# Splits, weight loads and zeros moved to other queues and places at four stage borders of a two-layer encoder kernel

## The chip, the cores and the metric

The kernel runs on one core of one Trainium2 chip. The metric is the device time of one execution in microseconds (us), taken as the median of several runs. A core has TensorE (PE, matmuls; PEld in the profile is its loading of the stationary operand), VectorE (DVE), ScalarE (ACT), GpSimd (POOL), and SyncE (SP), which only issues transfers (DMAs). Each engine works through its own queue of instructions in order and waits on semaphores for the others. Transfers issued by SP go to the queue that the profile calls q1, transfers issued by POOL to q0.

## The reference, cut to what matters

Two layers on x of 1024 tokens by 1024 channels, all in float32:

```
layer 0: h = LN(alpha*x + MLA(x));      h = LN(alpha*h + SwiGLU(h))
layer 1: h = LN(alpha*h + Diff(h));     h = LN(alpha*h + SwiGLU(h))

MLA:   c = x @ w_in; two RMS norms; q, k, v from the latents, a shared rotary key
       o = softmax(mask(q k^T * scale)) v, 8 heads;   o @ w_o
Diff:  q, k, v = h @ w_in; per head two softmax maps of 64 channels each
       a = softmax_0 - lam * softmax_1;  o = RMSnorm(a v) * g_sub * (1 - lambda_init);  o @ w_o
SwiGLU: (silu(gate) * up) @ w_down, 2816 hidden channels
```

The mask is causal by chunks of 64 tokens, and the differential attention has a penalty by distance.

## The kernel before, in words

**Products.** Every float32 operand of a matmul is split in two parts: hi is the value rounded to the matmul's format, lo is the rest. A product is three matmuls, hi·hi, hi·lo and lo·hi (`mm3`, L140). The hi part is a cast on ACT, the lo part a subtraction on DVE, or on POOL for weights. So whatever enters a product passes ACT first and then DVE or POOL. `load_w` (L128) does it for a weight: a transfer by SP into a raw tile, the cast at L136, the subtraction at L137 (POOL, if nothing else is asked for).

**Order.** The program is written as a list of Python calls, and a framework's scheduler, which has a time model of its own, sets the final order of each engine's queue. Two things hold it: a priority for some calls, and `behind(i, j)`, which forces instruction i to stand after j on the same engine, without a semaphore.

**Stages**, in order of time in the profile:

- *Start* (L927 to L1028). x comes transposed, in quarters for the first two blocks of 128 tokens (`load_x`); the eight row blocks of w_in come one after the other (`load_w_in`, the first in two pieces). `project` multiplies them as they come: hq (384 columns, L979) and hk (320 columns, L980). `ones`, a 128x128 constant that norms use later, is written by DVE at L1033.
- *Attention A* (L1051 to L1178). 8 heads by 8 blocks of 128 query rows; the last head takes its blocks in another order (6, 7, 4, 5, 2, 3, 0, 1, `LAST_ORDER`). For each block: scores on PE (s_a), row bounds on DVE (mx_a, L219), the exponential on ACT (L222), scaling by the row sum on POOL (l_a, L1137), transposes on PE (pt_a), their split (pth_a on ACT, L243, ptl_a on DVE, L244), and the product with the values (o_a, L255). The result goes to DRAM (o_dr).
- *out_proj 0* (L278). Eight weights wo0_0 to wo0_7 by `load_w`, and for each of eight token blocks: `of` from DRAM (eight heads by 128 columns), its split oh and ol (L302 on ACT, L303 on DVE), 48 matmuls (zp_a), residual and layer norm. Most weights are loaded during the attention; wo0_6 and wo0_7 come last.
- *FFN 0* (L486 on), whose end has a layer norm per token block: rs_f on POOL (L180), y_f on DVE (L176, L183), and transposes xTp_f on PE for layer 1.
- *Attention B* (L1203 to L1383), which starts in the shadow of FFN 0's end. Its two softmax maps lie on the two halves of the partitions, and the query tiles (bq, ql) must be zero where the other map's half is. Six quarter tiles of 64x512 that are never written otherwise (of bq1, ql0 and ql1) are zeroed once, by POOL, which subtracts the bias tile bb from itself (L1219). Each block of scores is two maps; l_b is scaled on POOL (L1281) and combined on DVE (L1282).
- *Output projection 1* (class `OutProj`, L325), interleaved with the last head of attention B. Its weights were split earlier and lie in DRAM (w_dr, in the profile wo_dr). `begin_out` (L1369) makes the object two blocks ahead of the last head: it loads `of` of the first block (6), then issues on POOL six loads of 1 MB (wo1_0 to wo1_5) and four of 512 KB (heads 6 and 7, into buffers shared with other weights). `of` (L349) loads six heads of a token block (384 KB in pieces of 512 bytes) and splits them: ACT at L377, DVE at L378; then it loads the residual z. A list (L1375) says in which block of attention B each piece is called: `early` products of the first block in slots 2 to 4, `of` of the second block (7) in slot 4, its `early` products in slots 6 and 7.
- *FFN 1* and the end.

Of the kernel before, what the change touches and what calls it, by code (L numbers as in the profile page):

```python
# [9 lines left out]
F32 = mybir.dt.float32  # L10
F32R = mybir.dt.float32r
# [31 lines left out]
def trunk(  # L43
# [57 lines left out]

    mhalf = cst[:, 0:2]
# [4 lines left out]
    def f32(t):  # L107
        return t.bitcast(F32)
# [15 lines left out]

    def small(name, n=1):
        return sp.tile([P, 2], F32, tag="small", name=name, bufs=22)[:, :n]

    def load_w(src, cols, name, hi=None, lo=None, eng=None, raw=None):  # L128
# [7 lines left out]
        A.copy(hi[:, :cols], raw[:, :cols])  # L136
        (eng or G).tensor_tensor(lo[:, :cols], raw[:, :cols], f32(hi[:, :cols]), ALU.subtract)  # L137
        return hi, lo
# [67 lines left out]
    def softmax_block(lp, q_pass, s_bias, i, scale, name):  # L206
        n = (i + 1) * P
        nb = 1 if n <= 512 else 2
        w = n // nb
        l = lp.tile([P, 1024], F32, tag="l", name=f"l_{name}")  # L210
        mx = BIGF
        for b in range(nb):
            s = ps_s(f"s_{name}_{b}")
            ks = slice(b * w, (b + 1) * w)
            for j, (lh, rh) in enumerate(q_pass):
                T.matmul(s[:, :w], lh, rh[:, ks], start=(j == 0), stop=(j == len(q_pass) - 1))
            bv = s_bias[:, 896 - P * i + b * w:896 - P * i + (b + 1) * w]
            m = small(f"mx_{name}_{b}")
            V.tensor_tensor_reduce(l[:, ks], s[:, :w], bv, -scale, mx, ALU.add, ALU.min, m)  # L219
            mx = m  # L220
        sm = small(f"sm_{name}")
        A.activation(l[:, :n], l[:, :n], AF.Exp, bias=mx, scale=-1.0, accum_out=sm)  # L222
        r = small(f"r_{name}")
        V.reciprocal(r, sm)  # L224
        return l, r

    def transpose_block(ptp, pts, l, i, name):
        qc = (i % 2) * P
        for jq in range(i // 4 + 1):
# [5 lines left out]
            for jp in range(2 * jq, 2 * jq + (nj + 1) // 2):  # L235
# [7 lines left out]
                A.copy(hv, src)  # L243
                V.tensor_tensor(lv, src, f32(hv), ALU.subtract)  # L244
# [33 lines left out]
    def out_proj(side, w_o, o_dram, x_src, x_dst, lng, lnb, xo):  # L278


        with tc.tile_pool(name="op0", bufs=2, side=side, reuse_waits="tile") as pool:
# [3 lines left out]
            for h in range(H):  # L285
# [7 lines left out]
                wo.append(load_w(w_o[h], 1024, f"wo0_{h}", *dst))  # L293
            prev = None
            for tb in LAST_ORDER:
# [6 lines left out]
                A.copy(oh, of)  # L302
                V.tensor_tensor(ol, of, f32(oh), ALU.subtract)  # L303
# [21 lines left out]
    class OutProj:  # L325
# [5 lines left out]
        def __init__(self, side, w_dr, o_dram, o_here, x_src, x_dst, scale):  # L331
# [4 lines left out]
            self.of(LAST_ORDER[0])  # L336
            self.wo = []
            for h in range(H):
                if h < self.HEADS:
                    t = self.pool.tile([P, 2, D], F32R, tag=f"wo{h}", name=f"wo1_{h}", bufs=1)  # L340
                    nc.gpsimd.dma_start(t, w_dr[h])
# [566 lines left out]

    o_dr = [[dr.tile([H, P, 256], F32, name=f"o_dr{l}_{g}") for g in range(4)] for l in range(2)]
    wo_dr = [dr.tile([P, 2, D], F32, name=f"wo_dr{h}") for h in range(H)]  # L910
# [122 lines left out]
    V.memset(ones, 1.0 / P)  # L1033
# [17 lines left out]
    with ast as st:  # L1051
# [76 lines left out]
        def score_a(h, i):  # L1128
# [8 lines left out]
            G.tensor_scalar(l[:, :n], l[:, :n], r, 1.0, ALU.mult, ALU.mult)  # L1137
# [39 lines left out]
        at(12, make_late)  # L1177
        attention(score_a, turn_a, mix_a, fill, 2, (0, 0))  # L1178
# [24 lines left out]
    with ExitStack() as st:  # L1203
# [11 lines left out]
        for ql in q_lo:  # L1215
            for mp in range(2):
                b = slice(64 - mp * 64, 128 - mp * 64)
                z = bb[b, :512]
                G.tensor_tensor(ql[b, mp * 512:mp * 512 + 512], z, z, ALU.subtract)  # L1219
# [258 lines left out]
```

## Time and profile before

| what | value |
|---|---|
| median of 3 runs | 2318.11 us (2317.43 to 2320.41) |
| the profiled execution, all of it | 2317.24 us |
| its span, first to last instruction | 2315.5 us |
| PE busy | 2253.4 us, 97% of the span |
| DVE, ACT, POOL busy | 67%, 44%, 39% |
| DMA queue of SP (q1) | 268.46 MB |
| DMA queue of POOL (q0) | 17.83 MB |

A row of a timeline gives the start and the length in us, engine and line, the operation, what it writes <- what it reads (buffer numbers left out: `wo` for wo1_3, and `s_b` for s_b7_7_0_0), the shape, how many such rows follow each other, and in brackets the idle time ahead of it and what ended it. "PE s_b <- DVE mx_b" reads: PE waited, ahead of a matmul into s_b, for DVE's mx_b. What ended a wait is inferred; where the named engine itself had been waiting for something, the cause lies one step further back.

### The profile page before, as it was taken

What the parts mean: (1) busy time and instruction counts of PE and PEld (TensorE: products, weight loads), DVE (VectorE), ACT (ScalarE), POOL (GpSimd) and SP (SyncE); (2) the same over time, 40 slices, a digit from 0 to 9 for tenths busy, and PEclk for the clock granted to TensorE, in tenths of its full rate; (3) what the DMA queues carried; (4) which work ended last, traced back from release to release, by engine and by line L of the source; (5) the groups of instructions that cost most, each with busy time, mean ns of one, the idle gap of its engine ahead of it and who ended that gap; (6) DMA issues with size and microseconds to landing.
All of it is one profiled execution on the core that took longest, in us unless ns stands there. A gap on an engine that the chain in (4) does not pass through costs nothing. (4 is left out here: it accounts for less than half of the span.)

```text
span 2315.5 us, 31126 instructions
## 1 busy us (share of the span) xinstructions
PE 2253.4 (97%) x11410; PEld 1918.7 (83%) x11410; DVE 1560.1 (67%) x2879; ACT 1018.5 (44%) x2092; POOL 891.9 (39%) x698
## 2 busy tenths in 40 slices
PE   9999999999999999999999999979999999999997
PEld 9898897888888887888888898967778888887886
DVE  5666664596666658677476766666596656658777
ACT  4466673352332324345465656545442333324343
POOL 2233351014444445465332423222014444436564
PEclk9999999999999999999999999989999999999999
DMA  5121335334323238454310202153344222337453
GB/s 202 41 91 69 106 101 178 125 142 145 125 76 129 86 119 322 182 183 140 101 46 31 71 25 69 37 191 111 126 144 149 99 103 102 113 129 303 146 203 121
DMA packets 103658, 288.29 MB, mean 125 GB/s; under 512 B 8528, under 2 KB 31696, under 8 KB 93008
## 3 DMA queue, kind: packets, MB, share of 16 engines
q1 hardware_dynamic: 98064, 268.46, 33.0%
q0 software_dynamic: 5440, 17.83, 2.3%
q8 instruction: 90, 1.47, 0.3%
q14 instruction: 64, 0.52, 0.1%
HBM read 205.00 MB, written 77.07 MB: 122 GB/s over the span
## 5 line engine op out<-in xcount | busy, mean ns | idle before, releaser
L469 ACT CAST op_g<-gr 128x512 fp32r<-128x512 f32 x240 | 147.5, 622 | 411.0 <-PE gb L514 228.3
L470 POOL TENSOR_TENSOR op_g<-gr,op_g 128x512 fp32r<-128x512 f32 x104 | 145.8, 1407 | 303.6 <-DVE tmp L605 153.6
L470 DVE TENSOR_TENSOR op_h<-rh,op_h 128x512 fp32r<-128x512 f32 x154 | 162.8, 1088 | 67.6 <-ACT op_h L469 67.6
L514 PE MATMUL ga<-xh_m,op_g 128*128 128x512 f32 x512 | 168.0, 389 | 0.0
L469 ACT CAST op_h<-rh 128x512 fp32r<-128x512 f32 x154 | 93.0, 619 | 145.0 <-PE dx L782 37.5
L782 PE MATMUL dw<-op_w_t,op_h 128*128 128x512 f32 x660 | 151.4, 390 | 0.0
L782 PEld LDWEIGHTS dw<-op_w_t,op_h 128*128 128x128 f32 x660 | 123.6, 188 | 25.9 <-DVE op_h L470 0.4
L222 ACT ACTIVATE l_b<-l_b,mx_b 128x256 f32<-128x256 f32 (+7 forms) x128 | 99.6, 778 | 76.2 <-DVE mx_b L219 74.2
L1281 POOL TENSOR_SCALAR l_b<-l_b,r_b,cst 128x128 f32<-128x128 f32 (+3 forms) x64 | 52.8, 825 | 205.1 <-DVE r_b L224 196.1
L470 POOL TENSOR_TENSOR op_w_t<-tt,op_w_t 128x512 fp32r<-128x512 f32 x66 | 98.8, 1501 | 77.1 <-ACT op_w_t L469 77.1
L782 PE MATMUL dx<-op_w_b,op_h 128*128 128x512 f32 x528 | 122.7, 392 | 5.9 <-ACT op_w_b L469 3.9
L782 PEld LDWEIGHTS dx<-op_w_b,op_h 128*128 128x128 f32 x528 | 98.3, 188 | 29.9 <-ACT op_w_b L469 4.7
L514 PE MATMUL gb<-t4h_f,op_g 128*128 128x512 f32 x352 | 115.8, 390 | 3.0 <-DVE tmp L597 3.0
L514 PE MATMUL gc<-b22h_f,op_g 128*128 128x512 f32 x352 | 115.6, 389 | 1.6 <-ACT op_g L469 1.6
L470 DVE TENSOR_TENSOR op_g<-gr,op_g 128x512 fp32r<-128x512 f32 x136 | 109.5, 807 | 9.0 <-ACT op_g L469 8.8
L514 PE MATMUL gc<-t1h_f,op_g 128*128 128x512 f32 x352 | 115.5, 389 | 0.0
L514 PE MATMUL gb<-t3h_f,op_g 128*128 128x512 f32 x352 | 115.2, 389 | 0.0
L514 PE MATMUL gb<-t2h_f,op_g 128*128 128x512 f32 x352 | 114.8, 389 | 0.0
L514 PEld LDWEIGHTS ga<-xh_m,op_g 128*128 128x128 f32 x512 | 96.1, 188 | 19.9
L470 POOL TENSOR_TENSOR op_g<-s,op_g 128x512 fp32r<-128x512 f32 x40 | 55.3, 1382 | 143.6 <-ACT op_g L469 143.6
L143 PE MATMUL bp<-xT_f,h_wb 128*128 128x512 f32 x256 | 103.4, 404 | 0.0
L145 PE MATMUL bp<-xT_f,l_wb 128*128 128x512 f32 x256 | 101.8, 398 | 0.0
(375 smaller groups left out, 6788.4 us busy)
## 6 DMA issues: line engine op xcount, KB each, us to landing
gr<-in_w_gu SPq DMA_DIRECT2D x44, 1024.0 KB, 6.7
rh<-h_dr SPq DMA_DIRECT2D x28, 1024.0 KB, 5.3
h_dr<-sh SPq DMA_DIRECT2D x22, 1024.0 KB, 4.9
h_dr<-hp SPq DMA_DIRECT2D x22, 768.0 KB, 4.1
tt<-in_w_dn SPq DMA_DIRECT2D x22, 512.0 KB, 7.5
rh<-h_dr SPq DMA_DIRECT2D x14, 768.0 KB, 4.3
z<-xs_dr SPq DMA_DIRECT2D x16, 512.0 KB, 10.0
rw_b<-in_w_dn SPq DMA_DIRECT2D x8, 1024.0 KB, 8.7
```

The lines of the kernel that those rows point to most:

```text
L143: T.matmul(ps_out, lh, rh, start=(i == 0), stop=False)
L145: T.matmul(ps_out, ll, rh, start=False, stop=(i == n - 1))
L222: A.activation(l[:, :n], l[:, :n], AF.Exp, bias=mx, scale=-1.0, accum_out=sm)
L469: A.copy(hi, src)
L470: eng.tensor_tensor(lo, src, f32(hi), ALU.subtract)
L514: T.matmul(o, w[:, a, kc], x[b][:, k, :], start=(first and k == 0 and (a, b) == (0, 0)), stop=(k == 3 and a == 1), skip_group_check=True,)
L782: T.matmul(o, h[:, a, c], w[:, b_], start=(first and (a, b_) == (0, 0)), stop=(last and a == 1), skip_group_check=True,)
L1281: G.tensor_scalar(l1[:, :n], l1[:, :n], r1, nlam, ALU.mult, ALU.mult)
```

## The change

1. *Start.* `ones` is written first thing on DVE. Eight matmuls of ones by ones into a score bank that nobody reads (`spin`) stand ahead of PE's first real matmul.
2. *End of attention A.* `load_w` can now hold the two halves of a split behind noted instructions: the splits of wo0_6 and wo0_7 stand behind the last exponential on ACT and the last scaling on POOL that were noted when the call was made. In out_proj 0 the split of each `of` is done in two halves of four heads, and those of the first block stand behind the last pth on ACT and the last ptl on DVE.
3. *Output projection 1.* `OutProj` loads `of` of both first blocks (6 and 7) before anything else, and all ten weight loads are issued by SP instead of POOL. The call of `of` for block 7 in slot 4 goes.
4. *Zeros.* In attention A (slot 14) ACT casts half a row of the zero part of ba into a tile, and SP stores it in DRAM (`zero_dr`). The six quarter tiles are filled by SP's transfers from there.

```diff
+    V.memset(ones, 1.0 / P)
...
+    def spin(n, name):
+        t = ps_s(name)
+        for i in range(n):
+            T.matmul(t[:, :P], ones, ones, start=True, stop=True)
...
+    newest = {}
+    def load_w(src, cols, name, hi=None, lo=None, eng=None, raw=None, after=()):
...
+        i = A.copy(hi[:, :cols], raw[:, :cols])
+        j = (eng or G).tensor_tensor(lo[:, :cols], raw[:, :cols], f32(hi[:, :cols]), ALU.subtract)
+        for k, key in zip((i, j), after):
+            behind(k.ins, newest[key])
...
-                wo.append(load_w(w_o[h], 1024, f"wo0_{h}", *dst))
+                wo.append(load_w(w_o[h], 1024, f"wo0_{h}", *dst, after=("exp", "scale") if h > 5 else ()))
...
-                A.copy(oh, of)
-                V.tensor_tensor(ol, of, f32(oh), ALU.subtract)
+                for hs in (slice(0, 4), slice(4, 8)):
+                    i = A.copy(oh[:, hs], of[:, hs])
+                    j = V.tensor_tensor(ol[:, hs], of[:, hs], f32(oh[:, hs]), ALU.subtract)
+                    if prev is None:
+                        behind(i.ins, newest["hi"])
+                        behind(j.ins, newest["lo"])
...
-            self.of(LAST_ORDER[0])
+            for tb in LAST_ORDER[:2]:
+                self.of(tb)
...
-                    nc.gpsimd.dma_start(t, w_dr[h])
+                    nc.sync.dma_start(f32(t), w_dr[h])
...
-                        nc.gpsimd.dma_start(t[p], w_dr[h][:, p])
+                        nc.sync.dma_start(f32(t[p]), w_dr[h][:, p])
...
+    spin(8, "spin0")
...
+        def store_zeros():
+            t = wp.tile([P, 1024], F32R, tag="wl", name="zeros")
+            A.copy(t[:, :512], ba[:, :512])
+            nc.sync.dma_start(zero_dr, f32(t[:, :512]))
+        at(14, store_zeros)
...
-                z = bb[b, :512]
-                G.tensor_tensor(ql[b, mp * 512:mp * 512 + 512], z, z, ALU.subtract)
+                nc.sync.dma_start(f32(ql[b, mp * 512:mp * 512 + 512]), zero_dr[b])
...
-            (4, "of", (second,)), (6, "early", (second, (0, 1, 2))), (7, "early", (second, (3, 4, 5))),
+            (6, "early", (second, (0, 1, 2))), (7, "early", (second, (3, 4, 5))),
```

`newest` notes the last instruction of a kind: "exp" at the exponential of `softmax_block`, "hi" and "lo" at the split in `transpose_block`, "scale" at POOL's scaling in attention A.

What this does to the queues, at three places. On SP where output projection 1 begins; before (of_a1_6 is the `of` of block 6; the weights stand on POOL):

```order
L1321 DMA o_dr1_3_88<-bo_10162 128x256
L354 DMA of_a1_6_15086<-o_dr1_3_88 128x6x128
L354 DMA of_a1_7_15420<-o_dr1_3_88 128x6x128
L354 DMA of_a1_4_15742<-o_dr1_2_87 128x6x128
L354 DMA of_a1_5_15833<-o_dr1_2_87 128x6x128
L372 DMA zy_a1_4_15747<-xs_dr1_98 128x1024
```

and after:

```order
L1346 DMA o_dr1_3_98<-bo_10191 128x256
L371 DMA of_a1_6_15115<-o_dr1_3_98 128x6x128
L371 DMA of_a1_7_15124<-o_dr1_3_98 128x6x128
L358 DMA wo1_0_15132<-wo_dr0_100 128x2048
L358 DMA wo1_1_15134<-wo_dr1_101 128x2048
L358 DMA wo1_2_15136<-wo_dr2_102 128x2048
L358 DMA wo1_3_15138<-wo_dr3_103 128x2048
L358 DMA wo1_4_15140<-wo_dr4_104 128x2048
L358 DMA wo1_5_15142<-wo_dr5_105 128x2048
L363 DMA who1_6_15144<-wo_dr6_106 128x1024
L363 DMA who1_7_15148<-wo_dr7_107 128x1024
L363 DMA wlo1_6_15145<-wo_dr6_106 128x1024
```

The ten weight loads have moved from POOL's queue into SP's, behind the second `of` and ahead of those of blocks 4 and 5.

On ACT at the end of attention A (pth_a7 are the last head's transposed weights, oh_a0_6 the first block's split of out_proj 0); before:

```order
L222 ACTIVATE l_a7_1_4545,sm_a7_1_4554<-l_a7_1_4545,mx_a7_1_0_4552 128x256
L136 CAST wo0_6_4670<-r_wo0_6_4671 128x1024
L243 CAST pth_a7_2_1_4541<-pt_a7_2_0_4533 128x128
L302 CAST oh_a0_6_4682<-of_a0_6_4680 128x1024
L243 CAST pth_a7_2_0_4537<-pt_a7_3_0_4559 128x2x128
L1147 COPY ob7_2_4516<-o_a7_2_4497 128x256
L243 CAST pth_a7_0_0_4586<-pt_a7_0_0_4584 128x128
L243 CAST pth_a7_0_0_4586<-pt_a7_1_0_4590 128x2x128
L243 CAST pth_a7_2_1_4541<-pt_a7_3_0_4559 128x2x128
L302 CAST oh_a0_7_4755<-of_a0_7_4753 128x1024
```

and after:

```order
L234 ACTIVATE l_a7_1_4558,sm_a7_1_4567<-l_a7_1_4558,mx_a7_1_0_4565 128x256
L146 CAST wo0_6_4683<-r_wo0_6_4684 128x1024
L146 CAST wo0_7_4688<-r_wo0_7_4689 128x1024
L255 CAST pth_a7_2_1_4554<-pt_a7_2_0_4546 128x128
L255 CAST pth_a7_2_0_4550<-pt_a7_3_0_4572 128x2x128
L1166 COPY ob7_2_4529<-o_a7_2_4510 128x256
L255 CAST pth_a7_0_0_4599<-pt_a7_0_0_4597 128x128
L255 CAST pth_a7_2_1_4554<-pt_a7_3_0_4572 128x2x128
L255 CAST pth_a7_0_0_4599<-pt_a7_1_0_4603 128x2x128
L315 CAST oh_a0_6_4695<-of_a0_6_4693 128x512 x2
L1166 COPY ob7_1_4594<-o_a7_1_4581 128x256
```

The first block's oh cast, now in two halves, has moved behind the last pth, and the cast of wo0_7 behind that of wo0_6. DVE's ol and ptl have moved alike, and on POOL both wo0 subtractions now stand behind the last l_a.

On POOL at the end of FFN 0; before:

```order
L137 TENSOR_TENSOR l_wb0_0_10304<-r_wb0_0_10301,h_wb0_0_10303 128x1024
L180 TENSOR_TENSOR rs_f0_0_10099<-ve_f0_0_10097,cst_63 128x1
L1219 TENSOR_TENSOR bq1_10159<-bb_10156 64x512 x2
L1219 TENSOR_TENSOR ql0_10163<-bb_10156 64x512 x2
L1219 TENSOR_TENSOR ql1_10164<-bb_10156 64x512 x2
L180 TENSOR_TENSOR rs_f0_1_10112<-ve_f0_1_10110,cst_63 128x1
```

and after:

```order
L147 TENSOR_TENSOR l_wb0_0_10333<-r_wb0_0_10330,h_wb0_0_10332 128x1024
L192 TENSOR_TENSOR rs_f0_0_10128<-ve_f0_0_10126,cst_63 128x1
L192 TENSOR_TENSOR rs_f0_1_10141<-ve_f0_1_10139,cst_63 128x1
L192 TENSOR_TENSOR rs_f0_2_10154<-ve_f0_2_10152,cst_63 128x1
L192 TENSOR_TENSOR rs_f0_3_10167<-ve_f0_3_10165,cst_63 128x1
```

The six zeros are gone from between the first and the second rs_f; SP's queue has six transfers in their place, two ahead of the load of bb and four behind it.

More of the change, by code (lines that the diff above doesn't have):

```diff
@@ L221, in softmax_block @@
         sm = small(f"sm_{name}")
-        A.activation(l[:, :n], l[:, :n], AF.Exp, bias=mx, scale=-1.0, accum_out=sm)
+        newest["exp"] = A.activation(l[:, :n], l[:, :n], AF.Exp, bias=mx, scale=-1.0, accum_out=sm).ins
         r = small(f"r_{name}")
@@ L242, in transpose_block @@
                 hv, lv = (t[:, :n, qc:qc + P] for t in pts[jp])
-                A.copy(hv, src)
-                V.tensor_tensor(lv, src, f32(hv), ALU.subtract)
+                newest["hi"] = A.copy(hv, src).ins
+                newest["lo"] = V.tensor_tensor(lv, src, f32(hv), ALU.subtract).ins
     def pv_group(pts, g, v_of, name):
@@ L907, in ffn @@
         return new, rest, normed
+    spin(8, "spin0")
     o_dr = [[dr.tile([H, P, 256], F32, name=f"o_dr{l}_{g}") for g in range(4)] for l in range(2)]
+    zero_dr = dr.tile([P, 512], F32, name="zero_dr")
     wo_dr = [dr.tile([P, 2, D], F32, name=f"wo_dr{h}") for h in range(H)]
@@ L1032, in trunk @@
     nlam = cst[:, 24:25]
-    V.memset(ones, 1.0 / P)
     lv = [late[:, 64 * i:64 * i + 64] for i in range(4)]
@@ L1136, in score_a @@
             n = (i + 1) * P
-            G.tensor_scalar(l[:, :n], l[:, :n], r, 1.0, ALU.mult, ALU.mult)
+            newest["scale"] = G.tensor_scalar(l[:, :n], l[:, :n], r, 1.0, ALU.mult, ALU.mult).ins
             lt[h, i] = l
```

3 lines of the change are left out of this document (removed).

## The prediction

> **What bounds the kernel now.** I read the page first, then the list of waits of TensorE, then the timeline of each engine around the longest waits, then the transfers there. The page's first part:
>
> ```profile
> PE 2253.4 (97%) x11410; PEld 1918.7 (83%) x11410; DVE 1560.1 (67%) x2879; ACT 1018.5 (44%) x2092; POOL 891.9 (39%) x698
> ```
>
> TensorE (PE) is busy 2253.4 of the span's 2315.5 us, so all its waiting is 62 us, and a change that leaves its matmuls alone can win only from that, or from time in which its clock is low. The waits, longest sums first (us in total, times, longest):
>
> ```profile
> PE s_b L216 <- DVE mx_b L219: 14.3, 1, 14.3
> PE hq L979 <- ACT wih L950: 4.3, 1, 4.3
> ...
> PE xTp_f L148 <- DVE y_f L183: 3.8, 2, 2.1
> ```
>
> These lie at places that the change touches; a fourth place, the end of attention A, has three waits that are shown below. Behind three of the four the granted clock is halved; the table of windows gives length, busy times of PE, its weight loads, DVE, ACT and POOL, the clock, DMA share and GB/s:
>
> ```profile
> 353.00:363.00 10.00, 8.54 (x28) 7.39 (x29) 2.76 (x6) 3.21 (x6) 2.51 (x2) 0.50 0.93 319
> 1536.20:1540.80 4.60, 4.59 (x11) 3.63 (x12) 3.19 (x9) 1.92 (x3) 1.08 (x1) 0.50 1.13 386
> 1110.70:1114.20 3.50, 3.43 (x12) 3.09 (x13) 3.50 (x7) 2.67 (x8) 0.00 (x0) 0.51 0.54 157
> ...
> 1518.00:1534.00 16.00, 3.42 (x12) 2.02 (x12) 2.47 (x7) 1.30 (x3) 3.52 (x6) 0.79 1.07 405
> ...
> 18.00:26.00 8.00, 8.00 (x51) 8.00 (x51) 3.34 (x13) 3.98 (x10) 1.13 (x2) 1.00 1.03 416
> ```
>
> At half clock half of the busy time is lost: 4.3, 2.3 and 1.7 us. The last two rows are the rates that the DMA engines reached, wanted below.
>
> **Output projection of layer B: -13.5 us.** The transfers (KB each, us from issue to landing) and the rows that wait for them:
>
> ```profile
> of_a<-o_dr SPq DMA_DIRECT2D x1, 384.0 KB, 3.5
> wo<-wo_dr POOLq DMA_DIRECT2D x1, 1024.0 KB, 5.9
> of_a<-o_dr SPq DMA_DIRECT2D x1, 384.0 KB, 18.8
> wo<-wo_dr POOLq DMA_DIRECT2D x1, 1024.0 KB, 16.9
> ```
>
> ```profile
> 1513.55 6.49 SPq L354 DMA_DIRECT2D of_a<-o_dr  x3
> 1513.82 3.25 POOL L341 DMA_DIRECT2D wo<-wo_dr  x6 [3.76 <-PE bp L145]
> 1532.79 0.93 ACT L377 ACTIVATE oh_a<-of_a,cst 128x768 fp32r<-128x768 f32 x1 [14.67 <-DMA of_a<-o_dr]
> 1519.83 0.71 PE L389 MATMUL zp_a<-wo,oh_a 128*128 128x512 f32 x2 [0.37 <-DMA wo<-wo_dr]
> 1536.21 0.79 PE L216 MATMUL s_b<-bk,bq 128*128 128x512 f32 x1 [14.30 <-DVE mx_b L219]
> ```
>
> PE's 14.30 us is put down to DVE, but the late thing is a transfer. The first `of` left SP at 1513.55 and took 3.5 us. The second left 0.4 us later, found six weights of 1 MB on POOL's queue, and took 18.8 us, to 1532.8, just when ACT's L377 starts. Behind L377 stand the casts and exponentials of the attention; behind its partner L378 on DVE stands mx_b. The place costs 0.37 + 14.30 us of waiting and 2.3 us of half clock: 17.0 us.
>
> Now both `of` leave first and all weights follow on SP. The first weight lands at 1513.82 + 5.9 = 1519.7 today, the sixth (the last of the x6, issued at about 1516.5, 16.9 us) at 1533.4: 2.74 us each. A second `of` ahead adds 0.4 MB: 1.0 us at 405 GB/s, 3.5 us if it took as long as the first by itself. I take 1.3, since transfers of one queue overlap: weight 0 at 1521.0 (1520.7 to 1523.2). PE wants it at 1519.83 - 0.37 = 1519.5: a new wait of 1.5 us (1.2 to 3.7) in place of 0.37. After that the product of weight 1, 2, 3, 4, 5 stands 7,424, 16,896, 24,832, 29,312 and 36,224 matmul columns behind that of weight 0 in the new order. At full clock 384 columns step 0.17 us (the rows of the start, below: 12.18 to 12.35), 0.42 to 0.44 ns each, so the products are due after 3.1, 7.0, 10.3, 12.2 and 15.1 us at the least. Weights at 2.74 us land after 2.7, 5.5, 8.2, 11.0 and 13.7: ahead, by 0.4 to 2.1 us. The `of` of the later blocks, which now stand behind ten weights on SP, are used only after the attention's end, and POOL is rid of its issues. I take 17.0 - 1.5 - 2.0 = 13.5, the 2.0 for what a wait near 1520 still does to the clock (1.7 after the wait of 2.1 at the end of FFN 0, below). Bounds: 15.5 (only the wait of 1.5) and 9 (a wait of 3.7, and 4.3 us for two half-clock spells and a late weight).
>
> **End of attention A: -6.5 us.** ACT, POOL, DVE and PE in turn:
>
> ```profile
> 347.04 1.05 ACT L136 CAST wo<-r_wo 128x1024 fp32r<-128x1024 f32 x1
> ...
> 349.01 1.04 ACT L302 CAST oh_a<-of_a 128x1024 fp32r<-128x1024 f32 x1 [0.76 <-DMA of_a<-o_dr]
> ```
>
> ```profile
> 349.92 2.33 POOL L137 TENSOR_TENSOR wo<-r_wo,wo 128x1024 fp32r<-128x1024 f32 x1
> ```
>
> ```profile
> 350.09 3.24 DVE L303 TENSOR_TENSOR oh_a<-of_a,oh_a 128x1024 fp32r<-128x1024 f32 x1 [1.51 <-ACT oh_a L302]
> ...
> 356.83 1.23 DVE L303 TENSOR_TENSOR oh_a<-of_a,oh_a 128x1024 fp32r<-128x1024 f32 x1 [2.29 <-ACT oh_a L302]
> ```
>
> ```profile
> 350.38 0.39 PE L255 MATMUL o_a<-pth_a,vh 128*128 128x256 f32 x1 [1.70 <-ACT pth_a L243]
> ...
> 353.72 0.58 PE L255 MATMUL o_a<-ptl_a,vh 128*128 128x256 f32 x1 [2.73 <-DVE ptl_a L244]
> ...
> 358.35 0.80 PE L143 MATMUL zp_a<-wo,oh_a 128*128 128x512 f32 x1 [0.73 <-ACT ob L1147]
> ```
>
> ACT's L302 waits for a transfer ahead of the last pth casts; DVE's L303 comes ahead of the last ptl, and takes 3.24 us where its twin takes 1.23, since POOL's subtraction runs until 352.25. Waits of 1.70 + 2.73 + 0.73 and 4.3 us of half clock make 9.5 us. In the new order the oh splits stand behind the last pth and ptl. What stays: two wo casts now stand together on ACT (1.05 us each, from 347.0) ahead of the next pth, so PE waits some 0.9 us at 348.7; and POOL's two wo subtractions run on end, from about 348.1 to 352.8 (2 x 2.33), under the first half of DVE's oh subtraction, which then ends at about 353.4 (half of 1.23 later). PE reaches zp near 352.1 (358.35 less 0.73, 2.73, 0.8 of the 1.70, and 2 us of half clock), does two matmuls and waits for that half: about 0.9 us. With 1.2 us for smaller handovers and a clock that may dip there, 3.0 us stay and 6.5 go. Bounds: 8.5 (only 1 us stays) and 4 (3 us stay and 2.5 us of half clock besides).
>
> **End of FFN 0: -4.5 us.**
>
> ```profile
> 1102.67 6.21 POOL L1219 TENSOR_TENSOR ql<-bb 64x512 fp32r<-64x512 f32 x4
> 1108.85 1.06 POOL L180 TENSOR_TENSOR rs_f<-ve_f,cst 128x1 f32<-128x1 f32 x2
> ```
>
> ```profile
> 1099.56 2.17 DVE L183 SCALAR_TENSOR_TENSOR y_f<-y_f,rs_f,gb_f 128x1024 f32<-128x1024 f32 x1 [1.51 <-POOL rs_f L180]
> ...
> 1103.62 0.20 DVE L178 TENSOR_SCALAR ve_f<-ssq_f 128x1 f32<-128x1 f32 x1
> ...
> 1109.43 1.28 DVE L183 SCALAR_TENSOR_TENSOR y_f<-y_f,rs_f,gb_f 128x1024 f32<-128x1024 f32 x1 [2.42 <-POOL rs_f L180]
> ```
>
> ```profile
> 1110.77 1.54 PE L148 MATMUL xTp_f<-ident,y_f 128*128 128x128 f32 x6 [2.14 <-DVE y_f L183]
> ```
>
> POOL's zeros stand between the first rs_f and the second. DVE's first L183 runs beside them and takes 2.17 us instead of 1.28; the second waits until POOL comes to its rs_f at 1108.85, though its input ve_f was ready at 1103.8. PE waits 1.7 and 2.14 us and then loses 1.7 at half clock: 5.5 us. Without the zeros on POOL the second y_f is ready by about 1106, ahead of PE's need at 1108.6, so 2.14 + 1.7 go, and 0.9 of the first wait. What is late next is the first rs_f, still behind POOL's l_wb: 0.8 us stays. I take 4.5 (2.5, if another half-clock window follows, to 5.5). The six transfers of 128 KB leave SP around the load of bb, far ahead of the scores that read them, where transfers of that size land in about 2 us:
>
> ```profile
> o_dr<-bo SPq DMA_DIRECT2D x24, 128.0 KB, 1.8
> ```
>
> The store of the zeros in attention A is one half-row cast on ACT (44% busy): nothing.
>
> **Start: -1.5 us.**
>
> ```profile
> 0.89 0.17 DVE L1033 MEMSET ones<- 128x128 f32 x1
> ```
>
> ```profile
> 5.73 0.63 PE L980 MATMUL hk<-wih,xh 128*128 128x320 f32 x1 [0.79 <-ACT wih L950]
> 6.16 0.52 PE L979 MATMUL hq<-wil,xh 128*128 128x384 f32 x1
> 6.48 0.52 PE L979 MATMUL hq<-wih,xl 128*128 128x384 f32 x1
> ...
> 12.18 0.34 PE L979 MATMUL hq<-wih,xh 128*128 128x384 f32 x1
> 12.35 0.31 PE L980 MATMUL hk<-wih,xh 128*128 128x320 f32 x1
> ```
>
> A 384-column matmul steps 0.32 us at first and 0.17 at 12.18. The second matmul waits for data until 5.73, so for nearly all of the 6 us from there PE runs cold and could win up to 3 us; about half of that I count, since the first weights come at DMA's pace (the 416 GB/s above is the queue's best) and faster matmuls would wait for some of them. The eight spin matmuls (fp32, two passes of 128 columns each: from the six transposes of 1.54 us above, about 0.21 us a pass) make 16 x 0.21 = 3.4 us, from 1.1, when ones is written, to 4.5 (today ones is written third on DVE, now first): they delay the first matmul (4.25) a little and the second not at all. I take 1.5, between 2.1 (the data hold PE back for a third of it) and 0. The Trainium skill's page "TensorE: Matmul & The Clock Gate", Part 1, says that the clock goes up after about 3.4 us of activity in a free-running window. By that rule 3.4 us of spinning fill a window only when its phase happens to fit, and this term would be anywhere between none and all, differently in each run; the trace's 6 us of cold matmuls agree with a window of such a length just missed.
>
> **The sum.** 13.5 + 6.5 + 4.5 + 1.5 = 26.0 us. The other rows that the order moves (layer B's heads 2 and 7, partial sums in the FFN) I cost at 0, within 1 us. The profiled execution took 2317.24 us (span 2315.5 and 1.74 around it), 0.87 below the median of 2318.11. 2317.24 - 26.0 + 0.87 = 2292.1: I say 2292. PE is busy nearly throughout between these places, so what one stage wins is not waited for in the next. The bounds sum to 15.5 and 31.6: 2303 and 2286.
>
> **Rivals.**
> - *The waits that stay keep the clock low* (0.15). At each of the three places 1 to 3 us of waiting stay. Today the half clock follows waits of 2.14 us (1.7 lost) as it does waits of 14. If each leaves one more half-clock window than I allow, 3 x 1.7 = 5 us come back: 2297. The Trainium skill, same page and part, has the clock drop after an idle window of about 3.4 us; by that rule waits of this length would cost nothing more. The trace does not agree: the longest single wait before 1110.7 is 2.14 us, and the clock there is 0.51.
> - *Only the transfers' order helps* (0.08): if DVE and POOL still get in each other's way at the two other places, and the spin misses, 13.5 us alone are won: 2304.6.
> - *SP serves the weights more slowly than POOL did* (slower, 0.03). If one weight took t us, the wait for the first grows by t - 2.5, that for the sixth by 5t - 15.1, and the matmuls between run at half clock, 8 us more: 6t - 9.6. At t = 6.5 this equals the 17.0 us that go here and the 12.5 of the other places; from 7.3 the kernel is over 0.2% slower; at 8 (one at a time, over twice the 3.5 us of a 0.4 MB `of`) it is 38.4 against 29.5: 9 us slower, 2327. Against it: SP's queue drew 416 GB/s at 18 to 26 us, 2.5 us for 1 MB.
> - *The second `of` is slow by itself* (0.03): its pieces are 512 bytes. If it took 18.8 us alone, the weights would queue behind it, and this place would win nothing: 2317.2 - 12.5 + 0.9 = 2305.6. Against it: the first took 3.5 us.
>
> My forecast has 0.69; 0.02 is for anything else. 0.2% is 4.6 us, about what the measurement can tell from no change (the three runs span 3 us). Faster 0.95, within 0.2% 0.02, slower 0.03. The range, 2285 to 2304, takes in the bounds and the first rival.
>
> **What would show it.** Right: ACT's L394 (L377 before) and PE's s_b without a wait of over 3 us near 1490; the second `of` at under 6 us; POOL without 64x512 rows and no wait of xTp_f over 1 us; the first zp_a of out_proj near 353 less what the start wins; steps of 0.17 us before 9 us. Wrong: weights of the last projection landing over 3 us apart with PE waiting for each; half-clock windows that move instead of going; a new wait at the last head's softmax that gives back more than 3 us.

## The result, and the profile after

| | before | after |
|---|---|---|
| median of 4 runs | 2319.26 us (2317.43 to 2321.85) | 2294.7 us (2293.21 to 2295.28) |
| ratio | | 0.9892 (0.9879 to 0.9906) |
| span of the profiled execution | 2315.5 us | 2293.2 us |

The kernel is faster by 1.1%, 24.6 us between the medians. The page's first part, after:

```profile
PE 2251.4 (98%) x11426; PEld 1918.7 (84%) x11426; DVE 1560.4 (68%) x2887; ACT 1018.6 (44%) x2101; POOL 877.9 (38%) x682
```

PE still does the same work (16 passes more, the spin), and its idle time went from 62 to 42 us. To see where, I cut both spans at four matmuls that wait briefly in both kernels: an s_a near 96 us, a gb of FFN 0 near 500, a pt_b early in attention B near 1240, and the first xTp_a after output projection 1, near 1650 (the first where it starts, the others where the wait ahead of them begins).

| stretch of PE, us | before | after | difference | predicted |
|---|---|---|---|---|
| start, to s_a near 96 | 97.05 | 96.40 | -0.65 | -1.5 |
| attention A's end and out_proj 0 | 412.45 | 404.37 | -8.08 | -6.5 |
| FFN 0 and its end, to pt_b | 733.35 | 729.36 | -3.99 | -4.5 |
| attention B and output projection 1 | 426.00 | 416.09 | -9.91 | -13.5 |
| the rest | 646.65 | 646.98 | +0.33 | 0 |
| the span | 2315.5 | 2293.2 | -22.3 | -26.0 |

The list of waits of PE, after, longest sums first (us in total, times, longest). The waits for s_b (14.3 us) and for hq (4.3) are gone from its top. New there is zp_a with 3.7 us for a weight; pt_b, the transposes of attention B, had 2.6 us before (the longest 1.5) and has 3.3 now (the longest, in the last head, 2.2):

```profile
PE dx L799 <- ACT op_w_b L486: 3.9, 2, 2.0
PE zp_a L406 <- DMA wo<-wo_dr: 3.7, 1, 3.7
PE pt_b L160 <- DVE l_b L1307: 3.3, 2, 2.2
```

**Output projection 1.** The transfers (KB each, us from issue to landing), then SP's issues, then the rows that wait for them or no longer do:

```profile
of_a<-o_dr SPq DMA_DIRECT2D x1, 384.0 KB, 3.6
of_a<-o_dr SPq DMA_DIRECT2D x1, 384.0 KB, 4.3
wo<-wo_dr SPq DMA_DIRECT2D x1, 1024.0 KB, 8.4
gb<-in_ln_mix_g POOLq DMA_DIRECT2D x1, 512.0 KB, 7.3
gb<-in_ln_mix_b POOLq DMA_DIRECT2D x1, 512.0 KB, 10.7
```

```profile
1500.81 0.96 SPq L371 DMA_DIRECT2D of_a<-o_dr  x2
1501.82 2.95 SPq L358 DMA_DIRECT2D wo<-wo_dr  x6
```

```profile
1501.66 0.59 POOL L436 DMA_DIRECT2D gb<-in_ln_mix_g  x1 [4.34 <-PE s_b L228]
1505.55 0.94 ACT L394 ACTIVATE oh_a<-of_a,cst 128x768 fp32r<-128x768 f32 x1 [0.18 <-DMA of_a<-o_dr]
1510.38 2.05 PE L406 MATMUL zp_a<-wo,oh_a 128*128 128x512 f32 x4 [3.67 <-DMA wo<-wo_dr]
1559.40 0.41 PE L160 MATMUL pt_b<-ident,l_b 128*128 128x128 f32 x2 [2.22 <-DVE l_b L1307]
```

The second `of` lands in 4.3 us, where it took 18.8, and its cast on ACT waits 0.18 us, where it waited 14.67. But the first weight, issued at 1501.82, takes 8.4 us, and PE waits 3.67 for it. Beside it two loads of 512 KB are under way on POOL's queue, gb, the constants of the next layer norm. The windows (length, busy PE, PEld, DVE, ACT, POOL, clock, DMA share, GB/s) behind the waits of 3.67 and 2.22 us are at half clock; the place at the end of attention A that was at half clock before is at full clock:

```profile
1508.70:1515.50 6.80, 5.12 (x14) 3.95 (x15) 3.11 (x11) 1.88 (x5) 0.00 (x0) 0.50 1.02 410
1559.90:1563.30 3.40, 3.40 (x13) 2.92 (x12) 1.83 (x3) 1.73 (x5) 0.14 (x1) 0.50 0.03 7
353.00:363.00 10.00, 10.00 (x46) 8.24 (x45) 1.99 (x4) 2.65 (x5) 2.54 (x2) 1.00 1.04 349
```

**End of attention A.** POOL, DVE and PE in turn. PE reaches zp at 350.49; the waits of 1.70, 2.73 and 0.73 us have become 0.63 and 1.13:

```profile
346.97 4.71 POOL L147 TENSOR_TENSOR wo<-r_wo,wo 128x1024 fp32r<-128x1024 f32 x2
349.61 3.24 DVE L316 TENSOR_TENSOR oh_a<-of_a,oh_a 128x512 fp32r<-128x512 f32 x2
```

```profile
347.97 0.39 PE L267 MATMUL o_a<-pth_a,vh 128*128 128x256 f32 x1 [0.63 <-ACT pth_a L255]
350.49 0.45 PE L155 MATMUL zp_a<-wo,oh_a 128*128 128x512 f32 x1
...
352.30 0.50 PE L157 MATMUL zp_a<-wo,oh_a 128*128 128x512 f32 x1 [1.13 <-DVE oh_a L316]
```

**End of FFN 0.** The zeros are gone from POOL, DVE's y_f takes 1.29 us instead of 2.17, and of PE's waits of 1.7 and 2.14 us one of 0.82 is left:

```profile
1091.54 1.29 DVE L195 SCALAR_TENSOR_TENSOR y_f<-y_f,rs_f,gb_f 128x1024 f32<-128x1024 f32 x1 [1.52 <-POOL rs_f L192]
```

```profile
1092.88 0.44 PE L160 MATMUL xTp_f<-ident,y_f 128*128 128x128 f32 x2 [0.82 <-DVE y_f L195]
```

**Start.** The spin runs, but the real matmuls behind it still step 0.32 us, down to 0.17 only from 10.2 us on:

```profile
1.05 3.79 PE L131 MATMUL spin<-ones 128*128 128x128 f32 x16 [1.05 <-DVE cst L106]
...
5.22 0.52 PE L999 MATMUL hq<-wil,xh 128*128 128x384 f32 x1
5.54 0.52 PE L999 MATMUL hq<-wih,xl 128*128 128x384 f32 x1
6.56 0.69 PE L999 MATMUL hq<-wih,xh 128*128 128x384 f32 x1 [0.50 <-ACT xh L961]
...
10.85 0.33 PE L999 MATMUL hq<-wil,xh 128*128 128x384 f32 x1
11.02 0.31 PE L1000 MATMUL hk<-wil,xh 128*128 128x320 f32 x1
```

### The profile page after: what moved, and what is told of

It is laid out like the page before. It is cut to its first block, busy times and chain, and to the rows that moved or that the text cites. A ratio compares the mean times of both kernels' runs of the same rounds, so it can differ in the third digit from the quotient of the medians.

```text
span 2293.2 us, 31159 instructions
## 1 busy us (share of the span) xinstructions
PE 2251.4 (98%) x11426; PEld 1918.7 (84%) x11426; DVE 1560.4 (68%) x2887; ACT 1018.6 (44%) x2101; POOL 877.9 (38%) x682
```

## The experiments

All start from the changed kernel. The kernels e1 to e4, e5 to e8 and e9 to e12 ran on one chip each, and only those are compared in whole times. Their runs, and the same cuts of the span:

| kernel | median (runs), us | attention A's end | FFN 0 | attention B, output projection 1 |
|---|---|---|---|---|
| e1 weights on POOL | 2307.77 (2302.78 to 2310.97) | 404.32 | 728.94 | 427.66 |
| e2 splits free | 2299.82 (2299.5 to 2300.83) | 410.20 | 728.92 | 415.13 |
| e3 zeros on POOL | 2302.9 (2302.39 to 2304.71) | 405.72 | 735.53 | 415.73 |
| e4 gb on SP | 2293.1 (2289.55 to 2295.4) | 404.26 | 729.60 | 411.67 |
| e5 the changed kernel again | 2294.53 (2294.5 to 2298.49) | 404.25 | 728.75 | 415.13 |
| e6 wait filled | 2291.78 (2290.16 to 2294.75) | 405.44 | 728.57 | 413.64 |
| e7 gb on SP, weight 0 first | 2292.02 (2289.14 to 2293.17) | 404.29 | 729.02 | 412.11 |
| e8 no spin | 2301.92 (2298.5 to 2305.44) | 409.78 | 729.20 | 414.65 |
| e9 one spin matmul | 2295.0 (2294.48 to 2298.27) | 404.36 | 729.08 | 415.89 |
| e10 oh free | 2299.52 (2297.13 to 2302.88) | 410.78 | 728.86 | 416.23 |
| e11 wo0 free | 2294.42 (2292.67 to 2295.03) | 403.26 | 728.81 | 416.57 |
| e12 queue and fill | 2287.93 (2287.58 to 2292.83) | 403.24 | 728.78 | 410.03 |

The kernel before, on these chips: 2317.49 (2315.29 to 2319.4), 2319.72 (2318.32 to 2323.66) and 2320.0 (2316.22 to 2321.2).

### e1: the weights back on POOL, both `of` still first

```diff
-                    nc.sync.dma_start(f32(t), w_dr[h])
+                    nc.gpsimd.dma_start(t, w_dr[h])
...
-                        nc.sync.dma_start(f32(t[p]), w_dr[h][:, p])
+                        nc.gpsimd.dma_start(t[p], w_dr[h][:, p])
```

> The changed kernel, with the ten weight loads of output projection 1 issued by POOL again; both `of` still leave first on SP. Theory (queues): before the change the second `of` also left SP only 0.4 us after the first, so what made it late was the weights on the other queue, which take nearly all of the DMA engines' time beside pieces of 512 bytes. It lands 15 to 19 us after its issue again, PE waits about 14 us at s_b, and the time is 10 to 12 us above the changed kernel, 2304 to 2308. Rival (order of issue): it is enough that `of` is asked for early in the program; it lands within 6 us, PE waits under 4 us, 2293 to 2297.

The stage is 11.6 us longer than in the changed kernel, the ratio to before 0.996 (0.9947 to 0.9973). Transfers, ACT and PE:

```profile
wo<-wo_dr POOLq DMA_DIRECT2D x1, 1024.0 KB, 6.1
of_a<-o_dr SPq DMA_DIRECT2D x1, 384.0 KB, 19.7
```

```profile
1520.81 0.93 ACT L394 ACTIVATE oh_a<-of_a,cst 128x768 fp32r<-128x768 f32 x1 [15.56 <-DMA of_a<-o_dr]
1524.23 0.79 PE L228 MATMUL s_b<-bk,bq 128*128 128x512 f32 x1 [15.22 <-DVE mx_b L231]
```

The second `of` is issued as early as in the changed kernel, at 1501.11, ahead of five of the six weights (1501.33 to 1503.44), and takes 19.7 us all the same: the weights' queue counts, not who is issued first. With weights in the other queue it shares the DMA engines with them and lands after the last of the six; ahead of them in one queue it lands first.

### e2: no split held back

```diff
-                wo.append(load_w(w_o[h], 1024, f"wo0_{h}", *dst, after=("exp", "scale") if h > 5 else ()))
+                wo.append(load_w(w_o[h], 1024, f"wo0_{h}", *dst))
...
-                for hs in (slice(0, 4), slice(4, 8)):
...
+                A.copy(oh, of)
+                V.tensor_tensor(ol, of, f32(oh), ALU.subtract)
```

> The changed kernel without its second part: the wo0 splits and the first oh split stand where the scheduler puts them, oh whole. Theory: the end of attention A gives back what it won, about 8 us (waits of 1.7 + 2.7 + 0.7 and a half-clock stretch of about 10 us): 2301 to 2304. Rival: the other parts have moved the arrival of `of` against the attention so that the order there matters less; under 3 us come back, 2294 to 2298.

The stage is 5.8 us longer (410.20 against 404.37), and the ratio 0.9926 (0.9911 to 0.994). The two waits are back, 1.83 and 2.62 us:

```profile
349.78 0.39 PE L267 MATMUL o_a<-pth_a,vh 128*128 128x256 f32 x1 [1.83 <-ACT pth_a L255]
353.00 0.58 PE L267 MATMUL o_a<-ptl_a,vh 128*128 128x256 f32 x1 [2.62 <-DVE ptl_a L256]
356.69 0.74 PE L155 MATMUL zp_a<-wo,oh_a 128*128 128x512 f32 x1
```

But zp begins without the wait of 0.73 us that it had before, and the stage is still 2.25 us shorter than before: something else in the change helps here. e8 to e11 look for it.

### e3: the zeros back on POOL

```diff
-                nc.sync.dma_start(f32(ql[b, mp * 512:mp * 512 + 512]), zero_dr[b])
+                z = bb[b, :512]
+                G.tensor_tensor(ql[b, mp * 512:mp * 512 + 512], z, z, ALU.subtract)
...
-        at(14, store_zeros)
```

> The changed kernel with the six zero fills computed by POOL again (and no store of zeros). Theory (queue): rs_f of the second block stands behind them on POOL, PE waits 1.7 and 2.1 us for y_f and loses a half-clock window: 4 to 5.5 us come back, 2298.5 to 2300.5. Rival (contention only): only the slowed DVE operation counts (2.17 instead of 1.28 us), about 1 us, 2295 to 2296.5.

The ratio is 0.994 (0.9925 to 0.9954). The stage is 6.2 us longer, more than I had priced. PE's waits:

```profile
1093.33 0.44 PE L160 MATMUL xTp_f<-ident,y_f 128*128 128x128 f32 x2 [1.70 <-DVE y_f L195]
...
1101.34 1.92 PE L160 MATMUL xTp_f<-ident,y_f 128*128 128x128 f32 x8 [2.40 <-DVE y_f L195]
```

The two waits are 1.70 and 2.40 us, 3.3 more than the 0.82 of the changed kernel; behind each PE is at half clock for some 3.4 us (before: only behind the second), which makes 1.7 us each. 3.3 + 3.4 = 6.7. So the zeros do cost their place on POOL and not only a slower y_f beside them, and what they cost depends on whether one or two half-clock stretches follow.

### e4: the loads of gb in SP's queue, behind the weights

```diff
-                nc.gpsimd.dma_start(gb[:, i], src.partition_broadcast(P))
+                nc.sync.dma_start(gb[:, i], src.partition_broadcast(P))
```

> The changed kernel with the two loads of layer-norm constants of output projection 1 (gb, 512 KB each) issued by SP, behind the weights, instead of by POOL. Theory: these loads, which POOL issues at once now that no weights stand ahead of them, share the DMA engines with weight 0 and make it late; without them weight 0 lands about 7 us after the first `of` leaves instead of 9.4, PE waits 1.0 to 1.8 us for it instead of 3.67, the half-clock stretch of 6.8 us shrinks to 3.4 or none, and the time falls by 2.5 to 5 us, to 2290 to 2292.5. Rival: the two `of` in their small pieces, or the queue itself, set when weight 0 lands; the wait stays above 3 us, 2294 to 2295.5.

Weight 0 and the matmul that waits for it, and the same stretch of 9 us in the changed kernel and here (in two fences):

```profile
wo<-wo_dr SPq DMA_DIRECT2D x1, 1024.0 KB, 6.0
```

```profile
1507.21 1.17 PE L406 MATMUL zp_a<-wo,oh_a 128*128 128x512 f32 x4 [1.25 <-DMA wo<-wo_dr]
```

```profile
1504.00:1513.00 9.00, 4.89 (x15) 3.27 (x15) 7.68 (x18) 4.33 (x8) 1.04 (x1) 0.76 1.03 401
```

```profile
1504.00:1513.00 9.00, 7.22 (x35) 5.27 (x35) 8.04 (x21) 5.69 (x12) 0.77 (x2) 1.00 1.03 433
```

The DMA engines are full in both (1.03), so the weight is early only because gb is not beside it: 6.0 us instead of 8.4. The wait falls to 1.25 us and the half clock behind it goes. The stage is 14.3 us shorter than before, against 9.9 in the changed kernel and the 13.5 predicted (with this edit the scheduler also orders some of the later work there otherwise). The whole time shows it less: 2293.1, ratio 0.9899 (0.9883 to 0.9916), no better than the changed kernel's ratio, with runs 6 us apart. e7 is the better test.

### e5: the changed kernel once more, beside e6 to e8

> The changed kernel as it is, as the yardstick for the three others on the same chip. Both theories: 2293 to 2296, PE waits 3.4 to 3.9 us for weight 0, and a half-clock stretch of 3.4 or 6.8 us lies behind that.

2294.53, ratio 0.9892 (0.9877 to 0.9906). In its profile only 3.4 us behind weight 0 are at half clock, not 6.8; the half-clock stretch that the first profile has at 870 is gone, and one has appeared at 2068: the same program, with its half clock in other places.

### e6: the wait for weight 0 filled with matmuls

```diff
+            if (tb, nh, heads[0]) == (LAST_ORDER[0], 0, 0):
+                for i in range(12):
+                    f = T.matmul(m[:, :P], ones, ones, start=True, stop=True, skip_group_check=True)
+                    if i == 0:
+                        behind(f.ins, newest["b7_6_1"])
```

> The changed kernel with twelve matmuls of ones by ones (24 passes, about 2.6 us at full clock) into the bank of the first zp_a, right ahead of it, where PE waits 3.67 us for weight 0. They add nothing to the result. Theory (clock): the wait itself costs 3.67 us, and the half-clock stretch behind it 2.5 to 3 us more; PE's idling is what drops the clock, so with the wait filled the stretch is gone and the time falls by 2 to 3 us against the changed kernel, although nothing comes earlier. Rival: the clock falls for another reason, or the fill delays the first product as much as it saves: within 0.7 us of the changed kernel.

```profile
1506.77 2.84 PE L406 MATMUL zp_a<-ones 128*128 128x128 f32 x24
1510.06 1.17 PE L411 MATMUL zp_a<-wo,oh_a 128*128 128x512 f32 x4 [0.45 <-DMA wo<-wo_dr]
```

```profile
1506.00:1516.00 10.00, 9.19 (x56) 7.63 (x55) 8.34 (x22) 4.95 (x12) 1.10 (x1) 1.00 1.02 412
```

The weight comes hardly earlier (0.2 us against e5, counted from the cut near 1240), and still the stage is 1.5 us shorter than in e5 and 2.45 shorter than in the first profile. That is about half of the time that PE was busy at half clock there (3.4 and 5.1 us). The whole is 2.75 us shorter than e5, with ranges that overlap by 0.25 (2290.16 to 2294.75, 2294.5 to 2298.49). Apart from the fill, the order of the instructions is the same but for one copy on DVE and a few matmuls into o_b. So it was PE's idling that lowered the clock, and this second cost was about the 1.7 us a window that the prediction's first rival had.

### e7: gb on SP, and weight 0 between the two `of`

```diff
-            for tb in LAST_ORDER[:2]:
-                self.of(tb)
+            self.of(LAST_ORDER[0])
...
+                if h == 1:
+                    self.of(LAST_ORDER[1])
```

This is beside the edit of e4.

> The kernel with gb on SP behind the weights, and weight 0 between the two `of` on SP. Theory (one queue, in order): weight 0 lands about 6 us after the first `of` leaves, in place of 7.0, and the second `of` at about 6.5 in place of 4.6; PE's wait for weight 0 falls from 1.25 us to under 0.6, and no half-clock stretch follows; 2.5 to 5.5 us below the changed kernel on this chip. Rival: ACT and DVE now wait for the second `of` ahead of the exponentials of the last head, and that wait comes back to PE at s_b: 1 to 2 us there, and no gain over the kernel with gb on SP alone (0 to 3 us below the changed kernel).

```profile
1505.77 1.17 PE L407 MATMUL zp_a<-wo,oh_a 128*128 128x512 f32 x4 [0.37 <-DMA wo<-wo_dr]
```

The wait is 0.37 us, as before the change. The second `of` now comes a little late for ACT, but holds up PE nowhere by more than 0.6 us. 2292.02 against 2294.53 for e5 on the same chip, ranges apart: 2.5 us. Both edits together are worth that much; the profiles give the second nothing beyond the first (the stage takes 412.11 us here and 411.67 in e4).

### e8: no spin

```diff
-    spin(8, "spin0")
```

> The changed kernel without the eight matmuls of ones at the start. Theory (phase): the spin moves the end of the cold stretch by as much as its phase against the window allows, 0.2 to 1.7 us in the profiles so far, so without it the first attention block is reached 0.2 to 1.7 us later, about 1 us on average, and the median rises by 0 to 2 us. Rival 1: the spin always saves about 1.5 us or more. Rival 2: it saves nothing, since the data set the pace: 0 in the profile.

7.4 us slower than e5, far more than the 0 to 2 that were expected. At the start the s_a near 96 is reached at 97.40, in the 11 profiles with eight spins at 96.13 on average (95.23 to 98.13). 5.5 us lie at the end of attention A, against e5. The two profiled executions are 4.0 us apart in all; what else makes the medians differ by 7.4 stays open. PE and ACT there, and two transfers of ob:

```profile
356.71 0.79 PE L155 MATMUL zp_a<-wo,oh_a 128*128 128x512 f32 x1 [6.17 <-ACT ob L1165]
```

```profile
354.59 1.14 ACT L315 CAST oh_a<-of_a 128x512 fp32r<-128x512 f32 x2 [4.21 <-DMA of_a<-o_dr]
356.29 0.37 ACT L1165 COPY ob<-o_a 128x256 f32<-128x256 f32 x1 [0.56 <-DMA o_dr<-ob]
```

```profile
o_dr<-ob SPq DMA_DIRECT2D x1, 128.0 KB, 1.7
o_dr<-ob SPq DMA_DIRECT2D x1, 128.0 KB, 8.1
```

zp waits 6.17 us for a copy of the *attention's* last result out of its PSUM bank. By the addresses in the two programs the first zp of out_proj 0 has bank 0; without spin the last o_a7_0 lies in that bank too, with spin in bank 2. The copy stands on ACT behind the cast of the second block's `of`, which waits 4.21 us for its transfer, and then needs a free ob, of which there are two: for the last 0.56 us it waits for a store of 128 KB. That store takes 8.1 us while other transfers of its own queue and of POOL's keep the DMA engines full (share 1.04); another, some 6 us earlier, takes 1.7. In the changed kernel the store is as slow (8.3 us) and ACT copies o_a as late (356.58), but PE doesn't wait for it. Spin's tile is the first of the score tag to be asked for, and with that the tiles of the first PSUM pool take other banks.

### e9: one spin matmul in place of eight

```diff
-    spin(8, "spin0")
+    spin(1, "spin0")
```

> The changed kernel with one matmul of ones at the start instead of eight. Every engine's order is that of the kernel without spin, but the score banks are again the first that the program uses, as in the changed kernel, so the last o_a of attention A lies in bank 2 and the first zp_a of out_proj 0 in bank 0 (without any spin, and before the change, both lie in bank 0, and zp_a must wait until ACT has copied o_a out, which waits for a store to DRAM). Theory (banks): the wait of 6.2 us ahead of zp_a does not appear, zp_a starts near 350.5, and the time is within 2 us of the changed kernel, 2294 to 2297. Rival (clock): the eight matmuls are worth what the kernel without spin lost, 7 us, by warming the clock or by the scheduler's order; with one of them 2299 to 2304.

```profile
350.70 0.44 PE L155 MATMUL zp_a<-wo,oh_a 128*128 128x512 f32 x1
...
352.52 0.50 PE L157 MATMUL zp_a<-wo,oh_a 128*128 128x512 f32 x1 [1.14 <-DVE oh_a L316]
```

2295.0, ratio 0.9897 (0.9881 to 0.9914), as the changed kernel; the stage 404.36 as there. One matmul at 1 us does not bring the clock up (full clock starts at 10.5 us here), and in the traces of e8 and e9 every engine has the same order of instructions but for this matmul. What it changes is that the tile is asked for: the last o_a7_0 lies in bank 2 again. So the 5.5 us come from the banks.

### e10 and e11: one half of the held splits each

e10 frees the oh splits, and e11 those of wo0_6 and wo0_7:

```diff
-                for hs in (slice(0, 4), slice(4, 8)):
...
+                A.copy(oh, of)
+                V.tensor_tensor(ol, of, f32(oh), ALU.subtract)
```

> The changed kernel with the first block's oh split of out_proj 0 whole and not held; the wo0 splits stay held. In the new order its cast stands ahead of the last two pth on ACT, its subtraction ahead of the last two ptl on DVE. Theory: the subtraction lasts over 3 us beside POOL's wo0 subtractions, PE waits 2 to 3 us for ptl and loses some half clock: 2.5 to 5.5 us above the changed kernel, 2297 to 2300. Rival: holding the wo0 splits was what counted, and this costs under 1 us.

```diff
-                wo.append(load_w(w_o[h], 1024, f"wo0_{h}", *dst, after=("exp", "scale") if h > 5 else ()))
+                wo.append(load_w(w_o[h], 1024, f"wo0_{h}", *dst))
```

> The changed kernel with the splits of wo0_6 and wo0_7 not held; oh stays in halves and held. ACT's cast of wo0_7 stands ahead of a pth again, POOL's subtraction of wo0_7 ahead of the last l_a. Theory: l_a comes some 2 us later, PE waits 1 to 2 us for it, and about 1 us of that is given back by the earlier end of POOL's splits: 0 to 2 us above the changed kernel, 2294 to 2297. Rival: this part alone won most of what the second part of the change won, and 4 us or more come back.

e10 brings the waits back:

```profile
350.12 0.66 PE L267 MATMUL o_a<-pth_a,vh 128*128 128x256 f32 x2 [0.87 <-ACT pth_a L255]
353.08 0.58 PE L267 MATMUL o_a<-ptl_a,vh 128*128 128x256 f32 x1 [2.30 <-DVE ptl_a L256]
```

e10 is 4.5 us slower than e9 and 5.1 slower than e11, and its stage 6.4 longer than in the changed kernel. e11 loses nothing: 2294.42, its stage even 1.1 us shorter (e12, which holds these splits, has the same 403.24). Holding oh back in halves is what the second part of the change wins; holding the weights' splits is worth nothing here. Holding oh and halving it were not tried apart.

### e12: what was learned, together

e7's edits, and a fill as in e6 ahead of the transposes pt_b of the last block, where PE waited 2.22 us:

```diff
+            if name == "b7_1":
+                for n in range(8):
+                    f = T.matmul(pt[:, :P], ones, ones, start=True, stop=True)
+                    if n == 0:
+                        behind(f.ins, newest["o_b7_1"])
```

> A version put together from what the runs showed: gb on SP behind the weights, weight 0 between the two `of`, and eight matmuls of ones into the bank of the last pt_b of attention B ahead of its transposes, where PE waits 2.2 to 2.5 us and a half-clock window follows (they add nothing to the result). Theory: 1 to 2 us below the kernel without the fill, 3.5 to 5 us below the changed kernel: 2289 to 2291.5. Rival: the fill only takes the place of the wait, and the half-clock window appears elsewhere: as without it, 2291 to 2293.

2287.93, ratio 0.9868 (0.9853 to 0.9883): 7.1 and 6.5 us faster than e9 and e11 on the same chip, more than the 3.5 to 5 expected, and the lowest ratio of all (e6 has 0.9877, well within the interval). The waits for weight 0 and for pt_b near the end are both gone, and the stage is 16 us shorter than before the change. What the fill alone did stays open: with it the scheduler also placed six products zp ahead of the last transposes, and that was not tried apart.

## Why the prediction was right, and where it was not

The forecast was 2292 (2285 to 2304), measured 2294.7: right in direction, 2.7 us too fast. The mechanism was right for the transfers of output projection 1 and for the zeros, half of it for the end of attention A, and it did not show at the start. That the number came so close is in part luck: terms that were too large (by 3.6, 0.9 and 0.5 us) stand against one that was too small (by 1.6), and that one was helped by a move of PSUM banks that was not seen; in e8, where this is absent, the median is 2301.92. By the terms of the sum:

- **Output projection 1, -13.5; measured -9.9.** That the second `of` is late because of the weights' queue is shown by the changed kernel (4.3 us) and, from the other side, by e1 (19.7). The mis-sized term is the new wait for weight 0: "1.5 us (1.2 to 3.7)" was 3.67, its upper end, and half clock took 2.6 us there (half of the 5.12 that PE was busy in the window) where 2.0 was allowed. 17.0 - 3.67 - 2.6 leaves 10.7; the wait for pt_b, which was not in the sum, takes 1.0 more than before (2.22 us and 1.7 of half clock, before the change 1.54 and 1.4), and 9.7 is within 0.2 of what was measured. The step that failed, behind the wait for weight 0, is "POOL is rid of its issues": the two loads of gb stay on POOL, and with no weights ahead of them they left at 1501.66, beside weight 0. I had taken weight 0's 5.9 us from a row of before, where the gb loads stood behind the weights. e4 puts gb behind them again and gets a wait of 1.25 and 14.3 us of gain in that stage.
- **End of attention A, -6.5; measured -8.1, by a mechanism of which I saw half.** The casts and subtractions ahead of the last pth and ptl were the cause of the two longer waits (e2, e10). Of the remainder, PE waits 0.63 + 1.13 us, less than the 3.0 allowed, and DVE's oh subtraction is as slow beside POOL (3.24 us) as predicted. But the wait of 0.73 for ob, which the sum took for a part of the same trouble, was one for a PSUM bank, and the spin moved that bank by accident. Alone, the held splits win 2.7 us at this place (e8) and the moved bank 2.25 (e2), and in both zp starts at 356.7; together they win 8.1, with zp at 350.5, since zp comes after the later of the two. An edit that I costed at the start of the kernel had its larger effect here, and that was luck. And the part on wo0_6 and wo0_7 is worth nothing (e11).
- **End of FFN 0, -4.5; measured -4.0, at the place itself 4.7** (waits of 3.8 us and 1.7 of half clock before, 0.82 after). Right, with the 0.8 left over that was named. e3, that part undone, costs 6.2 us in this stage and 7.9 in its span; of the remainder 1.8 us lie behind the last cut, where it has a half-clock stretch at 1678 and the changed kernel has none.
- **Start, -1.5; measured -0.65 here, -0.9 on average over the profiles with eight spins, from -1.8 to +1.1 in single ones.** A sign of being right that was named, steps of 0.17 us before 9 us, did not come in this profile, and the spin cannot be told from chance: e9, with one matmul, reaches s_a at 96.62, within the same spread. The Trainium skill's page "TensorE: Matmul & The Clock Gate", Part 1, describes a free-running window, by which the gain would vary from run to run; the profiles agree, as their full clock starts anywhere from 4.1 to 11.2 us. The clock is not all: the one profile at +1.1 (e5) is at full clock from 6.4 us on, but PE waits 1.75 us at 24.1 for an x that has come late.
- **The first rival, that waits that stay keep the clock low, holds in part.** The half clock follows the waits of 3.67 us and, near 1560, of 2.22; at the end of attention A and of FFN 0, where 1.13 and 0.82 us stay, it is gone. In e6 it goes with PE's idling, though the weight comes hardly earlier. The Trainium skill's page "TensorE: Matmul & The Clock Gate", Part 1, has the clock drop after an idle window of about 3.4 us; 2.22 us of waiting were enough here (1.70 in e3), so the measurement decides against that figure as a bound on a single wait.
- The other rivals fell: not only the transfers' order helps (8.1 and 4.0 us come at two other places), the `of` is not slow by itself (4.3 us), and SP serves the weights as fast as POOL (410 GB/s in the window at half clock).

## What to carry to other kernels

When a transfer is moved between queues, follow what is left in the queue that it leaves: the next transfer there starts earlier, and takes its share from the one that now has to be first. A wait of PE of 2 to 4 us can cost itself and 1.7 to 2.6 us more in half clock behind it, so it pays to end the last such wait at a place, or to fill it. And the first use of a tile can shift the banks of tiles that are used much later: before an edit is credited with a gain far from where it stands, run it with the same allocation and without its work.

## What had not been expected of the hardware

- Two queues share the DMA engines by something other than order of issue: 384 KB in pieces of 512 bytes took 19.7 us beside loads of 1 MB on the other queue, and 4.3 us ahead of them on the same one. A store of 128 KB took 8.1 us while loads of both queues kept the DMA engines full (e8), and 1.7 some 6 us earlier.
- Full DMA engines moved between 349 GB/s (share 1.04, the end of attention A) and 433 (share 1.03, e4).
- The half-clock stretches in the middle of these profiles are 3.4 us long or a multiple of it, each lies at a wait of PE of 1.5 us or more, and they move from execution to execution: the changed kernel had one at 870 in one profile and one at 2068 in the other. The length of the wait alone does not decide: the same wait of 1.95 us near 870 stands in all 14 profiles and has half clock behind it in 5 of them.
- Not every such stretch costs its 1.7 us. With the one near 870 the FFN 0 stage took 728.8 to 729.4 us in these 5 profiles, without it 728.6 to 729.6 in 7 others (before and e3 left aside): some 26 us behind that wait PE waits for data again, 0.9 to 1.9 us without the stretch and at most 0.7 with it, so the slower matmuls use up a wait. The stretch at 1678 in e3 does show (1.8 us). What part of the 1 to 8 us between runs of one kernel comes from this was not traced run by run.
